# A new order at the beginning of a two-block transformer kernel: mask matmuls ahead, first block by rows, x turned and memory normed behind it

## The chip, the cores and the metric

The kernel runs on one core of one Trainium2 chip. The metric is the device time of one execution in microseconds, the median over runs. Within the core the engines run side by side, each through its own queue in order: TensorE (PE; its weight loads are listed as PEld), VectorE (DVE), ScalarE (ACT), GpSimd (POOL) and SyncE (SP), whose queue here issues the DMAs from memory.

## The reference, cut to what matters

Two transformer blocks over 256 tokens of 1024 features, all in float32. The first block has a mixer of gated branches, a cross attention to a memory of 256 rows, and a mixture of experts; the second block has two more attention layers with rotary positions. The change touches only what stands at the very beginning:

```
h    = rmsnorm(x, norm_mix_g)
proj = h @ w_in                      # a_val, a_gate, u_pool, c_x, c_b, c_c, g
a    = a_val * sigmoid(a_gate)
a    = causal_dwconv(a, conv_a_w) + conv_a_b        # 31 taps
...
k, v = split(rmsnorm(mem, norm_mem_g) @ w_xkv, 2)   # cross attention, needs mem only
x    = x + mixer(h) ; x = x + cross_attention(...) ; x = x + moe(...)
...
cos, sin = rope_tables(positions)    # for the second block
cond     = silu(c)                   # for the second block
```

## The kernel before

Activations are kept with features on the 128 partitions and tokens along the row. Each float32 matmul is done as three matmuls of reduced-precision halves: a weight tile `raw` of 128x1024 comes by DMA, ACT copies it to its high half `whi` (line 99), DVE subtracts to get the low half `wlo` (line 100), and PE multiplies `whi` with the high and the low half of the activation and `wlo` with the high half (lines 141 to 143). A "block" below is one call of `fm_block`: 256 output features from 1024 inputs, 48 matmuls of 128x256, two weight tiles. In the beginning the halves are `hTh`/`hTl` for the normed x and `memTh`/`memTl` for the normed memory.

The order of the program before: x is loaded in two halves of 128 rows and normed (`norm_rows`, line 245 on: squares on ACT into `junk`, the inverse root on ACT and DVE, the scaling on DVE); h is transposed on PE and split into hTh and hTl (lines 554, 555); x itself is transposed as well and copied to `xT` (line 558), which the residual needs much later. Then 72 rows of gains are turned into columns (`gcols`), the memory is loaded, normed and turned by `to_fm` (lines 340 to 344) into memTh and memTl, the positions are loaded and cast (lines 574 to 576), sines and cosines are made, the convolution's 37 rows of constants are turned into `chv`, and four blocks of `w_in` follow. Blocks 1 and 2 give value and gate of the first half (`sg`, line 643, and `apad`, line 644), blocks 3 and 4 those of the second. Each pair starts a convolution `conv` (lines 630, 633), 62 DVE operations on `acv`, that is queued with `later` and stepped by `tick` at each further block. `xkv` then multiplies the normed memory with `w_xkv`.

What sets the order in each engine's queue is a scheduler in the framework: it takes the program in the order written, with the dependencies, priorities by program order and a model of durations, and writes one fixed instruction list for each engine; `behind` adds ordering edges without waits. On the chip nothing is reordered. Weight tiles `raw` and their halves each rotate through 6 buffers (lines 44, 45), the 128x1024 tiles x, h, memx, apad and cpad share four. DMA completions use eight semaphores in turn, so that a DMA is issued only when the eighth before it has landed.

## Time and profile before

| | |
|---|---|
| median of 3 runs | 1216.24 us (1214.25 to 1217.8) |
| profiled execution | 1219.56 us, of which the span is 1217.8 us |
| PE busy | 1175.7 us, 97% of the span |
| DVE busy | 887.5 us, 73% |
| ACT busy | 689.0 us, 57% |
| mean granted TensorE clock | 0.986 |

The profile's times are from the start of the span of one execution, so a row of its timeline can be set against a row of the same execution only. A row of the timeline gives the start, the length, the engine, the line and what is done; "xN" means that N such instructions follow each other and the length is that of all. Durations of neighbours on one engine overlap a little, so the distance of two starts is the better cost of one. In the profile's tables by window, the granted clock is 1.00 at the higher of its two levels (2.4 GHz) and 0.50 at the lower (1.2 GHz).

### The profile page before, as it was taken

How to read it: one execution, taken by the hardware profiler on the slowest of the kernel's cores; microseconds unless marked ns; L12 is line 12 of the kernel's file. 1: busy time of each engine (PE TensorE's matmuls, PEld its weight loads, DVE VectorE, ACT ScalarE, POOL GpSimd, SP SyncE). 2: the span in 40 equal slices, each digit the busy share in tenths (PEclk: the TensorE clock that was granted, in tenths of full speed). 3: DMA queues.
4: the chain of work that ended last, by engine and by line, in shares of the span. 5: the costliest groups of instructions: out<-in, count | busy, mean ns of one | idle time of the engine just before them, and what ended most of it. 6: DMA issues, size and time to landing. Idle time of an engine off the chain costs nothing.

```text
span 1217.8 us, 22374 instructions
## 1 busy us (share of the span) xinstructions
PE 1175.7 (97%) x8690; PEld 1056.2 (87%) x8690; DVE 887.5 (73%) x1649; ACT 689.0 (57%) x1149; POOL 30.7 (3%) x45
## 2 busy tenths in 40 slices
PE   7999999999989999899999999999999989999998
PEld 6989999989868888679667899999977758999998
DVE  7899977666479999697777695578489767654543
ACT  6554357554357777477466475455465555655543
POOL 0000000000000000070000000000010000000000
PEclk8999999999989999999899999999999999999999
DMA  8566565795458999684543597697665346756551
GB/s 253 168 213 190 168 209 167 227 344 184 130 191 286 343 325 359 244 245 161 168 146 122 182 378 240 195 319 268 218 210 182 97 138 208 242 177 196 184 173 36
DMA packets 161310, 258.27 MB, mean 212 GB/s; under 512 B 14255, under 2 KB 106247, under 8 KB 161196
## 3 DMA queue, kind: packets, MB, share of 16 engines
q1 hardware_dynamic: 161196, 256.76, 63.2%
q8 instruction: 70, 1.15, 0.4%
q14 instruction: 44, 0.36, 0.1%
HBM read 255.67 MB, written 1.05 MB: 211 GB/s over the span
## 4 chain that ended last, share of the span: by engine, by line
PE 64%; DVE 4%; DMA 2%; ACT 1%; issue 1%; DVEq 0%; ACTq 0%
PE fm L142 6%; PE fm L143 6%; PE fm L141 6%; PE mo L141 5%; PE mo L142 5%; PE mo L143 5%; PE tm L148 3%; PE tm L150 3%; PE tm L149 3%; PE gu L148 2%; PE gu L149 2%; PE gu L150 2%; PE ada L434 2%; DMA ada<-in_w_ada_dram 2%; PE o L1529 1%; PE py L148 1%
## 5 line engine op out<-in xcount | busy, mean ns | idle before, releaser
L100 DVE TENSOR_TENSOR wlo<-raw,whi 128x1024 fp32r<-128x1024 f32 (+1 forms) x383 | 457.5, 1217 | 167.3 <-ACT whi L99 163.1
L99 ACT ACTIVATE whi<-raw 128x1024 fp32r<-128x1024 f32 (+1 forms) x383 | 392.9, 1049 | 277.4 <-PE fm L142 144.0
L141 PE MATMUL fm<-hTh,whi 128*128 128x256 f32 (+1 forms) x968 | 272.3, 281 | 3.2 <-ACT hTh L217 3.2
L142 PE MATMUL fm<-hTl,whi 128*128 128x256 f32 (+1 forms) x968 | 272.6, 282 | 2.5 <-DVE hTl L555 1.6
L143 PE MATMUL fm<-hTh,wlo 128*128 128x256 f32 (+1 forms) x968 | 271.3, 280 | 0.8 <-DVE wlo L100 0.8
L141 PEld LDWEIGHTS fm<-hTh,whi 128*128 128x128 f32 (+1 forms) x968 | 181.9, 188 | 5.7 <-ACT hTh L217 4.6
L142 PEld LDWEIGHTS fm<-hTl,whi 128*128 128x128 f32 (+1 forms) x968 | 182.2, 188 | 4.6 <-DVE hTl L218 2.5
L143 PEld LDWEIGHTS fm<-hTh,wlo 128*128 128x128 f32 (+1 forms) x968 | 181.9, 188 | 1.1 <-DVE wlo L100 1.0
L142 PE MATMUL mo<-ul,whi 128*128 128x256 f32 x512 | 142.9, 280 | 0.0
L143 PE MATMUL mo<-uh,wlo 128*128 128x256 f32 x512 | 142.8, 280 | 0.0
L141 PE MATMUL mo<-uh,whi 128*128 128x256 f32 x512 | 141.6, 280 | 0.0
L143 PEld LDWEIGHTS mo<-uh,wlo 128*128 128x128 f32 x512 | 96.2, 188 | 0.0
L142 PEld LDWEIGHTS mo<-ul,whi 128*128 128x128 f32 x512 | 96.2, 188 | 0.0
L141 PEld LDWEIGHTS mo<-uh,whi 128*128 128x128 f32 x512 | 95.4, 188 | 0.4 <-issue 0.4
L148 PE MATMUL tm<-whi,hTh 128*128 128x512 f32 x176 | 69.3, 399 | 1.4 <-ACT hsq L907 0.7
L149 PE MATMUL tm<-wlo,hTh 128*128 128x512 f32 x176 | 69.1, 393 | 0.0
L150 PE MATMUL tm<-whi,hTl 128*128 128x512 f32 x176 | 68.0, 392 | 0.3 <-DVE hTl L218 0.3
L141 PE MATMUL fm<-oTh,whi 128*128 128x256 f32 x192 | 54.0, 285 | 2.4 <-ACT oTh L1708 1.4
L142 PE MATMUL fm<-oTl,whi 128*128 128x256 f32 x192 | 54.5, 285 | 0.9 <-DVE oTl L1709 0.8
L143 PE MATMUL fm<-oTh,wlo 128*128 128x256 f32 x192 | 53.1, 279 | 0.0
L633 DVE SCALAR_TENSOR_TENSOR acv<-apad,chv,acv 128x256 f32<-128x256 f32 x120 | 51.5, 478 | 0.0
L148 PE MATMUL gu<-whi,xgh 128*128 128x512 f32 x128 | 50.8, 398 | 0.0
(533 smaller groups left out, 2125.5 us busy)
## 6 DMA issues: line engine op xcount, KB each, us to landing
ada<-in_w_ada_dram SPq DMA_DIRECT2D x96, 512.0 KB, 5.9
raw<-in_w_mlp_in_dram SPq DMA_DIRECT2D x64, 512.0 KB, 6.1
raw<-in_w_mlp_out_dram SPq DMA_DIRECT2D x64, 512.0 KB, 4.3
raw<-in_w_in_dram SPq DMA_DIRECT2D x48, 512.0 KB, 5.1
raw<-in_w_e_down_dram SPq DMA_DIRECT2D x32, 512.0 KB, 4.6
raw<-in_w_e_gate_dram SPq DMA_DIRECT2D x62, 256.0 KB
raw<-in_w_e_up_dram SPq DMA_DIRECT2D x62, 256.0 KB, 4.9
raw<-in_diff_w_in_dram SPq DMA_DIRECT2D x24, 512.0 KB, 3.7
```

The costliest lines, as they stand in the source:

```text
L99: behind("A", SC.activation(hi[:, :n], raw[:, :n], AF.Copy))
L100: last["lo"] = behind("V", V.tensor_tensor(lo[:, :n], raw[:, :n], hi[:, :n].bitcast(F32), op=OP.subtract))
L141: T.matmul(ps, whi[:, c:c + ncol], xh[:, xk, :], start=first, stop=False, **kw)
L142: T.matmul(ps, whi[:, c:c + ncol], xl[:, xk, :], start=False, stop=False, **kw)
L143: return T.matmul(ps, wlo[:, c:c + ncol], xh[:, xk, :], start=False, stop=last, **kw)
L148: T.matmul(ps, xh[:, xk, t0:t0 + P], w[0], start=first, stop=False)
L149: T.matmul(ps, xh[:, xk, t0:t0 + P], w[1], start=False, stop=False)
L150: return T.matmul(ps, xl[:, xk, t0:t0 + P], w[0], start=False, stop=last)
L434: behind("T", T.matmul(ada_part["ps"][32 * j:32 * j + 32, :], w, r[:, S * j:S * j + S], start=start, stop=stop, skip_group_check=True))
L633: V.scalar_tensor_tensor(acv[:, f, :], apad[:, f, j:j + S], chv[:, f, j:j + 1], acv[:, f, :], op0=OP.mult, op1=OP.add)
L1529: T.matmul(o_[64 * hp:64 * hp + 64, :], vTM[:, a, s, gi, :], PT[hp, s, a], start=s == 0 and a == 0, stop=False, skip_group_check=True)
```

## The change

- 32 matmuls of 128x256 of the attention mask `cmask` with the bfloat16 identity, into a bank that nothing reads before it is overwritten, are put on PE ahead of everything else.
- The weight tiles of blocks 1 and 2 are all fetched ahead: one before the constants `col0`, the others right behind. Block 1's second tile is split only after half of hT.
- Block 1 is called with `first=True`: both halves of the output are accumulated row by row of the input (k outside, f inside), so that its first 6 matmuls need only the first row block of hT.
- x is turned into xT no longer ahead of block 1 but in two pieces by `residual`, queued with `later`, behind blocks 2 and 3; its transposes get `behind` edges (`turned` has a new argument `e` for that).
- The DMAs of the memory are written behind the loop over hT, and norm and turn of the memory (`memory`) behind block 1.
- The convolution's constants, `apad`, `conv` and the loop over the four blocks now stand ahead of `bcol`, the positions and sines.

The core of the diff:

```diff
+N_I = 32
...
+            for _ in range(N_I):
+                T.matmul(ada_bank[:, 0, :], identb, cmask, start=True, stop=True)
+            w0 = wmat(win, KD, 0, 256, 0, 1)
             c0_ = cols(16, "col0", vec("norm_mix_g"), vec("c_2"))
-            w0 = wmat(win, KD, 0, 256, 0)
+            w0.fetch(1)
+            w1 = wmat(win, KD, 512, 256, 0, 2)
             for t in range(2):
                 fence["V"] = norm_rows(xr[t], hs[t])
                 fence["A"] = fence["M"]
-            w0.load()
+            w0.load(1)
...
             for c in range(4):
+                if c == 2:
+                    w0.load(1)
                 ps = turned(hs, "hT", c)
...
-            for c in range(4):
-                V.tensor_copy(xT[:, 2 * c:2 * c + 2, :], turned(xr, "fm", c))
-            w1 = wmat(win, KD, 512, 256)
+            for t in range(2):
+                memx[t] = rowt("memx")
+                nc.sync.dma_start(memx[t], A["mem"][0, t * P:(t + 1) * P, :])
...
+            def residual():
+
+                yield
+                for c in range(4):
+                    V.tensor_copy(xT[:, 2 * c:2 * c + 2, :], turned(xr, "fm", c, "T"))
+                    if c % 2:
+                        yield
...
-            for t in range(2):
-                m = rowt("memx")
-                nc.sync.dma_start(m, A["mem"][0, t * P:(t + 1) * P, :])
-                norm_rows(m, m)
-                to_fm(m, aM, t, g_mem)
+            def memory(t):
+                norm_rows(memx[t], memx[t])
+                to_fm(memx[t], aM, t, g_mem)
...
+            for c in range(2):
+                pv = proj(c, None if c else w0, c == 0)
+                if c == 0:
+                    later(residual())
+                    for t in range(2):
+                        memory(t)
+                pg = proj(2 + c, None if c else w1)
+                sg = mx.tile([P, 2, S], F32, tag="sg", name="sg", bufs=4)
+                SC.activation(sg, pg, AF.Sigmoid)
+                V.tensor_tensor(apad[:, 2 * c:2 * c + 2, 30:30 + S], pv, sg, op=OP.mult)
+                later(conv(c))
             bcol = cols(96, "bcol", vec("b_ada_2"))
             pos_i = cp.tile([P, 2], I32, name="pos_i")
```

How the queues look now is shown at three places, before and after the change. First SP, from the first weights to the second set of them. Before, the positions' DMA is issued behind the first four weight tiles:

```order
L93 DMA raw<-in_w_in_dram 128x4x256 x4
L574 DMA pos_i<-in_positions_dram 128x2x1
L603 DMA rows<-in_conv_a_w_dram 31x512
L603 DMA rows<-in_conv_c_w_dram 3x512
L402 DMA rows<-in_norm_mem_g_dram 8x128
```

In the changed kernel the convolution's rows stand there, and the positions come later, behind three more weight tiles and ahead of the memory:

```order
L403 DMA rows<-in_ln_mix_g_dram 16x128
L403 DMA rows<-in_ln_mlp_g_dram 16x128
L593 DMA rows<-in_ln_a_g_dram 1x512
L593 DMA rows<-in_ln_a_b_dram 1x512
L94 DMA raw<-in_w_in_dram 128x4x256 x3
L642 DMA pos_i<-in_positions_dram 128x2x1
L569 DMA memx<-in_mem_dram 128x1024 x2
L861 DMA brt<-in_b_rg_dram 128x4
L94 DMA raw<-in_w_in_dram 128x4x256
L862 DMA brt<-in_b_re_dram 128x16
L94 DMA raw<-in_w_xkv_dram 128x4x256 x3
```

The positions moved from the 9th DMA to the 24th, and the memory from ahead of the second set of weights to behind its first three.

Second, DVE around the cast of the positions (`pos`), which is the instruction that waits for that DMA. Before, it stands behind block 1's two wlo:

```order
L100 TENSOR_TENSOR wlo<-raw,whi 128x1024 x2
L576 CAST pos<-pos_i 128x2
L555 SCALAR_TENSOR_TENSOR hTl<-hT,col_117,hTh 128x256 x3
L580 TENSOR_SCALAR ang<-pos 128x2 x8
L555 SCALAR_TENSOR_TENSOR hTl<-hT,col_117,hTh 128x256 x3
```

In the changed kernel:

```order
L565 SCALAR_TENSOR_TENSOR hTl<-hT,col_153,hTh 128x256
L597 COPY chv<-ax 128x4x37
L644 CAST pos<-pos_i 128x2
L101 TENSOR_TENSOR wlo<-raw,whi 128x1024
L648 TENSOR_SCALAR ang<-pos 128x2 x8
L101 TENSOR_TENSOR wlo<-raw,whi 128x1024 x2
```

The cast went behind the whole of hTl, and the wlo that follows it is now the first of block 2, whose third matmul reads it.

Third, DVE up to the last of the 16 memTl operations. Before, its last 12 rows up to there are:

```order
L100 TENSOR_TENSOR wlo<-raw,whi 128x1024
L630 TENSOR_SCALAR acv<-apad,chv 128x256 x2
L644 TENSOR_TENSOR apad<-fm,sg 128x2x256
L344 SCALAR_TENSOR_TENSOR memTl<-ax,gcols,memTh 128x128
L633 SCALAR_TENSOR_TENSOR acv<-apad,chv,acv 128x256 x2
L630 TENSOR_SCALAR acv<-apad,chv 128x256 x2
L633 SCALAR_TENSOR_TENSOR acv<-apad,chv,acv 128x256
L344 SCALAR_TENSOR_TENSOR memTl<-ax,gcols,memTh 128x128
L633 SCALAR_TENSOR_TENSOR acv<-apad,chv,acv 128x256 x5
L344 SCALAR_TENSOR_TENSOR memTl<-ax,gcols,memTh 128x128
```

In the changed kernel:

```order
L618 TENSOR_SCALAR acv<-apad,chv 128x256 x2
L621 SCALAR_TENSOR_TENSOR acv<-apad,chv,acv 128x256
L701 MEMSET sA 128x4x16
L408 COPY bcol<-ax 128x96
L621 SCALAR_TENSOR_TENSOR acv<-apad,chv,acv 128x256
L345 SCALAR_TENSOR_TENSOR memTl<-ax,gcols,memTh 128x128
L621 SCALAR_TENSOR_TENSOR acv<-apad,chv,acv 128x256 x5
L345 SCALAR_TENSOR_TENSOR memTl<-ax,gcols,memTh 128x128
L621 SCALAR_TENSOR_TENSOR acv<-apad,chv,acv 128x256 x5
L345 SCALAR_TENSOR_TENSOR memTl<-ax,gcols,memTh 128x128
L621 SCALAR_TENSOR_TENSOR acv<-apad,chv,acv 128x256 x5
L345 SCALAR_TENSOR_TENSOR memTl<-ax,gcols,memTh 128x128
```

Of the convolution's operations (acv) 12 stood ahead of the last memTl before, 4 on line 630 and 8 on line 633; now 29 do, 4 and 25. From the wlo that waits for the sine's neighbours on ACT to that last memTl, DVE's list in the changed kernel has 4 wlo, 2 copies to xT, 2 apad, 16 memTl, 29 acv and five small operations.

On ACT the loads of function tables are in another order: before, a table is loaded for sin, then for sgc (the sigmoid of c), and sg follows with that table; in the changed kernel tables are loaded four times in the same stretch, for sg, for r (an exponential, of the memory's norm), for sgc and for sin, and a fifth time for the second sg.

## Rows read from the trace of the kernel before

**Rows 1.** The page: the span, and busy time of PE with its share.

```profile
span 1217.8 us, 22374 instructions
...
PE 1175.7 (97%) x8690; PEld 1056.2 (87%) x8690; DVE 887.5 (73%) x1649; ACT 689.0 (57%) x1149; POOL 30.7 (3%) x45
```

**Rows 2.** Windows: length, PE, PEld, DVE, ACT, POOL busy (count), PE clock, DMA.

```profile
40.00:60.00 20.00, 20.00 (x170) 19.83 (x169) 17.89 (x42) 9.41 (x17) 0.00 (x0) 1.00 0.39 129
...
240.00:260.00 20.00, 20.00 (x180) 18.39 (x182) 9.59 (x14) 7.56 (x11) 0.00 (x0) 1.00 0.95 330
260.00:280.00 20.00, 18.55 (x165) 16.54 (x158) 16.90 (x24) 15.06 (x26) 0.00 (x0) 1.00 1.01 355
```

**Rows 3.** Windows by stage of the beginning.

```profile
12.70:17.20 4.50, 2.14 (x9) 1.67 (x9) 4.50 (x18) 1.92 (x5) 0.00 (x0) 0.57 0.23 65
17.20:20.20 3.00, 3.00 (x16) 3.00 (x16) 2.66 (x18) 2.00 (x4) 0.00 (x0) 0.51 0.85 257
...
31.60:34.41 2.81, 0.16 (x3) 0.04 (x1) 0.87 (x5) 2.78 (x7) 0.00 (x0) 0.89 1.09 348
34.41:37.20 2.79, 2.79 (x13) 2.79 (x14) 2.79 (x5) 2.10 (x5) 0.00 (x0) 0.50 0.62 200
...
47.30:55.00 7.70, 7.70 (x65) 7.70 (x66) 7.61 (x21) 2.10 (x5) 0.00 (x0) 1.00 0.45 145
```

**Rows 4.** Timeline of SP: start, time to issue, DMA.

```profile
4.62 2.29 SPq L574 DMA_DIRECT2D pos_i<-in_positions_dram  x1
...
14.51 0.32 SPq L402 DMA_DIRECT2D rows<-in_ln_mlp_g_dram  x1
...
16.83 2.54 SPq L93 DMA_DIRECT2D raw<-in_w_in_dram  x4
19.42 3.13 SPq L839 DMA_DIRECT2D brt<-in_b_rg_dram  x1
```

**Rows 5.** A wait of SP's queue, 0 to 60 us: total, times, longest.

```profile
SPq L402 <- DMA rows<-in_conv_a_w_dram: 1.2, 1, 1.2
```

**Rows 6.** DMAs issued in 0 to 40 us: count, size, time to landing.

```profile
x<-in_x_dram SPq DMA_DIRECT2D x2, 512.0 KB, 3.5
...
pos_i<-in_positions_dram SPq DMA_DIRECT2D x1, 1.0 KB, 8.2
```

**Rows 7.** Timeline of ACT: start, length, instruction, idle before.

```profile
23.74 1.06 ACT L99 ACTIVATE whi<-raw 128x1024 fp32r<-128x1024 f32 x1 [0.54 <-DMA raw<-in_w_in_dram]
25.25 1.06 ACT L99 ACTIVATE whi<-raw 128x1024 fp32r<-128x1024 f32 x1 [0.44 <-DMA raw<-in_w_in_dram]
...
30.04 0.33 ACT L255 ACTIVATE r<-rv 128x1 f32<-128x1 f32 x2
30.39 1.28 ACT L597 ACT_TABLE_LOAD   x1
31.68 0.21 ACT L597 ACTIVATE sin<-ang 128x16 f32<-128x16 f32 x1
```

**Rows 8.** Timeline of DVE, the same columns.

```profile
14.10 0.17 DVE L576 CAST pos<-pos_i 128x2 f32<-128x2 int32 x1
...
35.41 2.35 DVE L100 TENSOR_TENSOR wlo<-raw,whi 128x1024 fp32r<-128x1024 f32 x2
37.68 0.69 DVE L644 TENSOR_TENSOR apad<-fm,sg 128x512 f32<-128x512 f32 x1
...
38.61 1.59 DVE L344 SCALAR_TENSOR_TENSOR memTl<-ax,gcols,memTh 128x128 fp32r<-128x128 f32 x6
...
51.39 0.73 DVE L630 TENSOR_SCALAR acv<-apad,chv 128x256 f32<-128x256 f32 x2
...
52.69 2.06 DVE L633 SCALAR_TENSOR_TENSOR acv<-apad,chv,acv 128x256 f32<-128x256 f32 x5
54.67 0.34 DVE L344 SCALAR_TENSOR_TENSOR memTl<-ax,gcols,memTh 128x128 fp32r<-128x128 f32 x1
```

**Rows 9.** Timeline of PE: first matmul of xkv, and the first that reads memTl's last row.

```profile
47.34 0.28 PE L141 MATMUL fm<-memTh,whi 128*128 128x256 f32 x1
...
55.25 0.28 PE L142 MATMUL fm<-memTl,whi 128*128 128x256 f32 x1
```

## What the change was predicted to do, before it ran

> **What bounds the kernel now.** I read the page first: PE is busy for 1175.7 of 1217.8 us [rows 1], so the time is PE's work plus the places where PE stands. Then the windows of 20 us: from 40 to 260 us PE shows 20.00 of 20.00 in each of the eleven (the first and the last stand in [rows 2]). So a delay or a gain made in the beginning arrives undiminished at 260 us; in the next window 1.45 us are idle, at a DMA share of 1.01, and over the whole span 42.1 (the difference of the two numbers of the page), the beginning's own with them. The change is worth what it does to the moment at which PE enters its long unbroken stretch.
>
> That moment was read from windows cut by stage. Before, the beginning has three weak places [rows 3]: block 1 starts while hT is still being made (2.14 of 4.50 us busy, granted clock 0.57, then 3.00 us at 0.51); PE stands 2.65 us for the memory's norm; and the 13 instructions behind that run at 0.50. From 47.30 to 55.00 PE is full, and DVE too (7.61 of 7.70). This last row decides: xkv starts at 47.34, the last memTl is computed from 54.67 to 55.01, and the matmul that reads it starts at 55.25 with no idle time before it [rows 8, 9]. DVE delivered it just in time. So I ask when the last memTl comes in the changed kernel, whatever PE gains ahead of it.
>
> **The mask matmuls and block 1 by rows.** The trace has no such matmul of bfloat16. From below they cost nothing (PE waits for x then anyway); from above, 32 matmuls at the distance that fp32r matmuls of this size have at the lower clock: 16 instructions in 3.00 us [rows 3], 0.19 each, 6.0 us. I take 6: from about 2 to 8 us. They may raise the clock by then, but h is ready only after them, so the clock may fall again. x's transposes and copies leave the stretch before block 1, its tiles are split earlier and it needs only one row block of hT to begin: I put its start 1.5 us earlier, at about 11.2, and its end between 20 (all at the higher clock and paced by hTl) and 22, against 23.8 before. Either value is without effect if the next step is right.
>
> **The positions.** DVE's list has the cast of the positions ahead of block 2's first wlo. Before, the cast took 0.17 us and found its data landed [rows 8]; the DMA had been issued at 4.62 and taken 8.2 us, so it landed at 12.8: 1 KB took as long as the four weight tiles queued ahead of it [rows 4, 6]. Now it is the 24th DMA. SP's chain: ln_mlp was issued at 14.51, one of two rows behind a wait for the 31 rows of the convolution [rows 4, 5]; these still land behind the first four tiles, so about 14.2 remains. Four rows of 0.3 to 0.4 us follow, then three weight tiles (4 took 2.54 us [rows 4], 0.5 to 0.6 each): 15.7 to 17.3. The positions' own issue takes 2.29 us: until 19.6. Three tiles of 512 KB are ahead of them, the first landing some 3 us behind its issue (x: 3.5 for two [rows 6]) and the others 1.5 us apart (ACT takes them up at 23.74 and 25.25, both times from a wait for the DMA [rows 7]): 18.8, 20.3, 21.8. The positions land at about 21.9; bounds 19.9 (at once when issued) and 24 (if 256 small pieces take as long again as the issue). The cast and the wlo behind it (2.35 for two [rows 8], so 1.2) end at 23.3. Block 2 was ready to start at 20 to 22 and does its third matmul at 23.3. With 46 matmuls at 0.118 us (65 in 7.70 [rows 3]) block 2 ends at 28.7; 30.8 if the clock is low for a while.
>
> **The sigmoid and the tables.** The first sg stands on ACT behind the whi of a tile of block 3, whose DMA can be issued only when the wlo above has released a buffer, and behind `brt`, 3.13 us of issue [rows 4]: memory's two DMAs until 20.4, `brt` until 23.5, a tile, and then this one at 24.4. It lands at about 28: 21.8 plus four transfers of 1.5 (two of memory, a tile and its own). With whi 1.06, two small operations, 0.6, and a table load of 1.28 [rows 7], sg starts at G = 31.0 to 31.3; bounds 29 and 33. I take 31.3. Behind it on ACT: sg 0.6 (taken a little below apad's 0.69, which has the same size [rows 8]), whi 1.05, load 1.28, r 0.33, load and sgc 1.5, load and sin 1.5, and the first of two whi 1.0. The wlo that DVE does next waits for that whi: G + 7.2 = 38.5. Until then DVE has only the memory's norm left to do, and PE block 3 and the transposes.
>
> Three loads are new in the program. In the trace a load costs its own 1.28 us: r ends at 30.37, the load starts at 30.39, and sin starts at 31.68 [rows 7]. The Trainium skill ("ScalarE: Activation LUTs", section "What ACT_TABLE_LOAD costs") gives 1283 ns for the load and 1380 ns of drain with it, 2.66 us for each switch. By that the four loads up to this point would cost 5.5 us more and the sum would be 1228.5; this trace shows the load's part to within 0.01 us and no drain around it.
>
> **DVE up to the last memTl.** From 38.5 on nothing on DVE's list should wait: what it reads from PE and ACT comes earlier. The work, by distances in [rows 8]: 4 wlo at 1.14 to 1.17, 4.6; two xT copies and two apad at 0.62 (the next row of DVE behind apad), 2.5; 16 memTl at 0.265 (six in 1.59), 4.2; 4 acv of line 630, 0.73 for two less the overlap, 1.3; 25 acv at 0.40 (five in 2.06), 10.0; five small operations, 0.5. Sum 23.1: the last memTl ends at 61.6 instead of 55.01. That is 6.6 us later. The 17 more acv operations that stand ahead of it explain 17 x 0.40 = 6.8 of that by themselves.
>
> PE meanwhile: block 3 from 31.9, the memory's transposes at 38.4, block 4 from 40.3 (its first bank is free when xT is copied) to 46, xkv from there, with the 65 matmuls that don't need the last row until 53.7. So PE enters xkv 1.3 us earlier than before, with 0.85 us of small transposes still to do inside it, and then waits some 7 us in a few pieces, since each of the last three memTl stands behind five acv. Behind the waits nothing gives it back: the acv done early are DVE work saved later, but PE isn't short of DVE there [rows 2]. **Sum:** 6.6 plus 0.2 for the same pick-up as before is +6.8 us. On the profiled execution's 1219.56 that is 1226.4; on the median, 1216.24, which I predict against, **1223.0**. Bounds: G at 29 gives +4.5; G at 33 gives +8.5, and if the clock is at its lower level behind PE's waits, as it was for 2.79 us behind the stall before [rows 3], 1.4 us for each of two such places come on top: +11.3, 1227.5.
>
> **Rivals.**
> 1. *Faster, about 1208.* The three weak places vanish: 25 instructions at 0.118 instead of 7.5 us, less what hTl's pace keeps, 4.1; the stall of 2.8; 1.3 from transposes at full clock [rows 3]. That is 8.2 us. It needs the last memTl at 47, or at 51.6 for a gain of 0.3%; by DVE's 30.3 us from G, that is G at or below 21.3. For it: PE's weak places are real and the program addresses each. Against it: raw tiles that land at 1.5 us each and the positions behind them put G eight us later.
> 2. *No change, about 1216.* Landings are earlier than I think and the small DVE operations cheaper, so that the last memTl comes at about 55 (G at 24.7), or PE's later waits take up the shift. Against it: the bound of 29 for G, and only 1.45 us idle in the first window that has any [rows 2].
> 3. *Slower still, about 1228 to 1232*: the positions land at 24 or later and a low clock follows each wait, or each table load holds ACT for longer than its own 1.28 us, say as long again: four of them are 5.1 us, 1228.1. [Rows 7] speak against the second. The page of the Trainium skill named above says about that much.
> 4. *The mask matmuls don't do what they are for*: done at 8 us, the clock is back at the lower level when block 1 starts. That costs 2 to 3 us in block 1 and nothing in the sum, as PE waits for DVE until 23.3 in any case.
>
> **How the numbers follow.** My forecast (with 4 in it) 0.66, rival 1 0.12, rival 2 0.16, rival 3 0.06. A measurement of this kernel can tell 0.3%, 3.65 us, from no change. The forecast's own range, 1220.7 to 1227.5, lies above 1219.9, with 0.02 of its chance left below that; so slower has 0.64 + 0.06 = 0.70, the same 0.16 + 0.02 = 0.18, and faster 0.12. The range leaves out rival 1's deeper gains and most of rival 3: 1212.5 to 1228.5.
>
> **What would show it.** In the profile after: a wait of DVE for the positions' DMA ahead of a wlo near 22 us, and PE waiting for that wlo at block 2's third matmul; table loads four times between about 29 and 37; PE idle inside xkv, released by memTl, three times or more, 6 to 8 us in all, and the last memTl at about 61.5. If the cast doesn't wait, or G lies before 27, the chain is wrong at its start; if the last memTl comes at 55 or earlier, it is wrong in DVE's sum. A PE that is full in xkv would refute it.

## The result, and the profile after

The changed kernel takes 1227.21 us (median of 6 runs, 1225.59 to 1229.88); the kernel before 1215.53 (6 runs, 1211.51 to 1220.67). The two medians lie 11.7 us apart. The ratio that the text goes by is not their quotient (1.0096) but 1.0077, with a 95% interval of 1.0056 to 1.0097: slower by about 9.4 us. The profiled executions differ by 8.07 (1227.63 against 1219.56). The forecast was 1223.0 with a range of 1212.5 to 1228.5, and slower at 0.70.

The page of the kernel after; to be set against [rows 1]. The span grew by 8.1 us and PE's busy time by 3.9, but the masks' 5.1 us are in the busy time, in a stretch in which PE waited for x for about half of the time before. Without them PE is busy for 1.2 us less than before, so the loss is PE standing and not PE working for longer:

```profile
span 1225.9 us, 22435 instructions
...
PE 1179.6 (96%) x8722; PEld 1058.0 (86%) x8722; DVE 887.7 (72%) x1649; ACT 693.1 (57%) x1152; POOL 30.7 (3%) x45
```

Windows of the kernel after, with the columns of [rows 2]. The window 40 to 60, which was full, now has 3.51 us idle, and the next one 1.81. The idle time at 260 to 280 is 1.45 us as before: nothing is given back there.

```profile
40.00:60.00 20.00, 16.49 (x131) 15.32 (x130) 19.66 (x51) 10.97 (x24) 0.00 (x0) 1.00 0.38 125
60.00:80.00 20.00, 18.19 (x147) 17.70 (x147) 20.00 (x42) 9.82 (x13) 0.00 (x0) 1.00 0.34 104
...
260.00:280.00 20.00, 18.55 (x174) 15.15 (x174) 12.03 (x23) 11.51 (x23) 0.00 (x0) 1.00 0.96 334
```

What matters is when xkv is through. The next row is the list of one tile's instructions (memTh) on PE: one of xkv's three matmuls in each step, with the shortest, median and longest duration in ns, then the start of the first and of the last. First the kernel before:

```profile
L141 PE MATMUL fm<-memTh,whi x64: 280/283/283, 47.3 to 70.0; 128*128 128x256 f32 x64
```

Then the kernel after:

```profile
L142 PE MATMUL fm<-memTh,whi x64: 278/283/387, 49.2 to 79.1; 128*128 128x256 f32 x64
```

So xkv starts 1.9 us later and lasts 29.9 us instead of 22.7; its last step comes 9.1 us later. Of the longer 7.2 us, 5.0 are PE's waits for sg and memTl. The rest is in part the four transposes of memx put in between (0.60 us) and the slower first matmul behind each wait; I didn't break it down further. PE's timeline of the kernel after shows the masks, block 2's third matmul and two of xkv's waits (start, length, instruction, idle time before it and what ended it):

```profile
2.13 5.12 PE L537 MATMUL ada<-cmask,identb 128*128 128x256 bf16 x32 [2.13 <-DVE identb L386]
...
26.17 0.58 PE L144 MATMUL fm<-hTh,wlo 128*128 128x256 f32 x1 [5.39 <-DVE wlo L101]
...
52.60 0.39 PE L142 MATMUL fm<-memTh,whi 128*128 128x256 f32 x1 [1.40 <-ACT sg L635]
...
64.24 0.39 PE L143 MATMUL fm<-memTl,whi 128*128 128x256 f32 x1 [0.91 <-DVE memTl L345]
```

The list of waits, 0 to 70 us, gives the sums (total, times, longest):

```profile
DVE pos L644 <- DMA pos_i<-in_positions_dram: 6.1, 1, 6.1
...
PE fm L143 <- DVE memTl L345: 3.6, 5, 0.9
```

DVE's timeline of the kernel after, which answers to [rows 8]: the cast that waits for the positions, the wlo behind it, the memory's scaling, the wlo from which the sum ran, and the last convolution ahead of the last memTl.

```profile
24.81 0.17 DVE L644 CAST pos<-pos_i 128x2 f32<-128x2 int32 x1 [6.09 <-DMA pos_i<-in_positions_dram]
24.89 1.23 DVE L101 TENSOR_TENSOR wlo<-raw,whi 128x1024 fp32r<-128x1024 f32 x1
...
39.07 0.17 DVE L671 TENSOR_TENSOR cond<-col,sgc 128x8 f32<-128x8 f32 x1 [1.26 <-ACT sgc L670]
...
39.46 1.67 DVE L260 TENSOR_SCALAR memx<-memx,r 128x512 f32<-128x512 f32 x4
...
41.55 1.23 DVE L101 TENSOR_TENSOR wlo<-raw,whi 128x1024 fp32r<-128x1024 f32 x1 [0.34 <-ACT whi L100]
...
61.85 2.07 DVE L621 SCALAR_TENSOR_TENSOR acv<-apad,chv,acv 128x256 f32<-128x256 f32 x5
63.83 0.36 DVE L345 SCALAR_TENSOR_TENSOR memTl<-ax,gcols,memTh 128x128 fp32r<-128x128 f32 x1
```

ACT's row for the third of the three tiles that are fetched ahead of the positions, then its row for the whi ahead of sg, then ACT between sg and the whi for which that wlo waits: the four loads and what they stand ahead of.

```profile
24.14 1.06 ACT L100 ACTIVATE whi<-raw 128x1024 fp32r<-128x1024 f32 x1 [2.49 <-DMA raw<-in_w_in_dram]
...
31.62 1.06 ACT L100 ACTIVATE whi<-raw 128x1024 fp32r<-128x1024 f32 x1 [1.63 <-PE fm L143]
...
33.07 1.28 ACT L635 ACT_TABLE_LOAD   x1
34.37 0.60 ACT L635 ACTIVATE sg<-fm 128x512 f32<-128x512 f32 x1
...
35.93 1.28 ACT L256 ACT_TABLE_LOAD   x1
37.22 0.29 ACT L256 ACTIVATE r<-rv 128x1 f32<-128x1 f32 x2
37.54 1.28 ACT L670 ACT_TABLE_LOAD   x1
38.83 0.21 ACT L670 ACTIVATE sgc<-col 128x8 f32<-128x8 f32 x1
39.06 1.28 ACT L665 ACT_TABLE_LOAD   x1
40.35 0.22 ACT L665 ACTIVATE sin<-ang 128x16 f32<-128x16 f32 x1
```

SP's queue up to the positions (start, time to issue; to be set against [rows 4]), and then windows: the transfers between 11 and 17 us, and the two stretches at the lower clock, block 1's beginning and block 2 behind the wait.

```profile
10.28 0.27 SPq L403 DMA_DIRECT2D rows<-in_norm_f_g_dram  x1
11.75 0.27 SPq L403 DMA_DIRECT2D rows<-in_pool_scale_dram  x1
14.00 0.32 SPq L403 DMA_DIRECT2D rows<-in_ln_mix_g_dram  x1
...
15.44 1.49 SPq L94 DMA_DIRECT2D raw<-in_w_in_dram  x3
16.97 0.52 SPq L642 DMA_DIRECT2D pos_i<-in_positions_dram  x1
17.58 0.94 SPq L569 DMA_DIRECT2D memx<-in_mem_dram  x2
```

```profile
11.00:17.00 6.00, 5.75 (x33) 5.41 (x34) 4.52 (x11) 4.60 (x10) 0.00 (x0) 0.72 0.11 32
...
12.00:15.00 3.00, 2.87 (x14) 2.80 (x14) 2.65 (x6) 2.65 (x6) 0.00 (x0) 0.50 0.05 17
...
26.00:29.00 3.00, 2.83 (x13) 2.83 (x14) 3.00 (x13) 2.72 (x9) 0.00 (x0) 0.50 0.83 256
```

The last number of a window's row is GB/s: for six microseconds, in block 1, hardly anything was transferred (32). SP's rows show why: each small row is issued when the eighth DMA before it has landed. For the rows at 10.28 and 11.75 that is a weight tile, one every 1.5 us; for the row at 14.00 it is the convolution's 31 rows. All tiles issued so far had landed near 11, and the next one was issued at 15.44. The kernel before has this hole too, with 79 GB/s from 11 to 17 us.

### The profile page after: what moved, and what is told of

The parts are those of the page before. It is cut to its first block, busy times and chain, and to the rows that moved or that the text cites. A ratio compares the mean times of both kernels' runs of the same rounds, so it can differ in the third digit from the quotient of the medians.

```text
span 1225.9 us, 22435 instructions
## 1 busy us (share of the span) xinstructions
PE 1179.6 (96%) x8722; PEld 1058.0 (86%) x8722; DVE 887.7 (72%) x1649; ACT 693.1 (57%) x1152; POOL 30.7 (3%) x45
## 4 chain that ended last, share of the span: by engine, by line
PE 61%; DVE 5%; issue 2%; DMA 2%; ACT 2%; SPq 0%; DVEq 0%; ACTq 0%
PE fm L143 6%; PE fm L144 6%; PE fm L142 6%; PE mo L142 5%; PE mo L143 5%; PE mo L144 5%; PE tm L149 3%; PE tm L151 3%; PE tm L150 3%; PE gu L149 2%; PE gu L150 2%; PE gu L151 2%; PE ada L435 1%; DMA ada<-in_w_ada_dram 1%; DVE wlo L101 1%
```

## The experiments

Every kernel of the experiments ran beside the kernel before on the same chip. "xkv" is the start of the first and of the last of its 64 steps in the profile, as in the two rows above; it comes from a single profiled execution of each kernel. Such times differ by about 1 us between kernels whose lists are the same up to there: sg starts at 34.37 in the changed kernel and at 33.20 in conv_behind.

| run | xkv, us | last memTl starts | ratio to before, 95% interval |
|---|---|---|---|
| before | 47.3 to 70.0 | 54.67 | 1 |
| after | 49.2 to 79.1 | 63.83 | 1.0077 (1.0056 to 1.0097) |
| no_mask | 48.8 to 78.5 | 63.28 | 1.0086 (1.0059 to 1.0113) |
| pos_early | 48.7 to 78.7 | 62.80 | 1.009 (1.0062 to 1.0118) |
| mem_tables | 48.4 to 76.9 | 61.60 | 1.0062 (1.0043 to 1.008) |
| mem_late | 47.6 to 76.6 | 59.90 | 1.0054 (1.0033 to 1.0074) |
| conv_behind | 48.0 to 71.3 | 54.52 | 1.0041 (1.0022 to 1.006) |
| pos_conv | 50.1 to 73.3 | 56.34 | 1.0035 (1.0019 to 1.0052) |
| full | 48.0 to 71.2 | 53.54 | 1.0014 (1.0 to 1.0028) |
| full2 | 45.8 to 69.1 | 52.05 | 0.9997 (0.9982 to 1.0012) |
| full4 | 40.3 to 63.5 | 46.25 | 0.995 (0.993 to 0.9969) |
| full4_nomask | 41.7 to 64.9 | 47.63 | 0.9972 (0.9958 to 0.9986) |
| before_mask | 45.1 to 67.8 | 52.39 | 0.9995 (0.9978 to 1.0012) |
| before_small | 43.7 to 68.6 | 53.32 | 1.0007 (0.9995 to 1.0019) |

Divided by 1216, the shift of xkv's last step gives the ratio to within 0.2 points in 12 of the 13 rows (after: 9.1 us, 0.75%; mem_late: 6.6, 0.54%; full4: -6.5, -0.53%). Only conv_behind stands 0.3 points above it. In conv_behind and before_small the shift lies outside the ratio's interval. An early start of xkv counts for nothing by itself: before_small starts it 3.6 us earlier and takes 1.0007.

Four of the rows form a square. Putting the convolution behind memTl takes 0.36 points off the changed kernel (after to conv_behind) and 0.40 off mem_late (mem_late to full). The edits of mem_late, which put the memory ahead, take 0.23 off the changed kernel (after to mem_late) and 0.27 off conv_behind (conv_behind to full). Both together take 0.63 of the 0.77 points, about the sum of the two. The smaller steps by themselves are no wider than the intervals.

**1. The positions' DMA early (pos_early).** Only the place of that one DMA changes: from behind the second set of tiles to right behind the first four.

```diff
             w1 = wmat(win, KD, 512, 256, 0, 2)
+            pos_i = cp.tile([P, 2], I32, name="pos_i")
+            ...
+                nc.sync.dma_start(pos_i, ...)
...
             bcol = cols(96, "bcol", vec("b_ada_2"))
-            pos_i = cp.tile([P, 2], I32, name="pos_i")
-            ...
-                nc.sync.dma_start(pos_i, ...)
```

> The changed kernel with one edit: the DMA of the positions is issued right behind the first four weight tiles, as before the change. Theory A (a chain: the positions' landing holds DVE at the cast, so block 2, the first sigmoid and DVE's run to the last memTl all come later; then 29 convolution operations stand ahead of the last memTl): the cast no longer waits (6.1 us in the changed kernel), block 2 starts at about 20.8 without the 5.4 us of waiting, the first sigmoid starts near 30 instead of 34.4, the last memTl ends near 60 instead of 64.2, and the time is 3 to 4.5 us below the changed kernel's, about 1223. Rival B (the convolution ahead of memTl is all that counts, the cast's wait is hidden by DMA landings further on): the last memTl stays at 63 to 64 and the time within 1 us of the changed kernel's, 1226 to 1228. Rival C (the clock: block 2 and the waits inside xkv at a lower clock): time as in A only if the granted clock of 26 to 29 us, 0.50 in the changed kernel, is 1.00.

The cast ran at 12.95 us, PE's wait of 5.4 us at block 2 was gone, and sg started at 31.94 instead of 34.37. The time didn't get better: 1.009, as rival B said, though not for its reason. DVE's timeline and PE's waits in this run show what came next:

```profile
38.27 0.17 DVE L671 TENSOR_TENSOR cond<-col,sgc 128x8 f32<-128x8 f32 x1 [2.88 <-ACT sgc L670]
...
62.80 0.35 DVE L345 SCALAR_TENSOR_TENSOR memTl<-ax,gcols,memTh 128x128 fp32r<-128x128 f32 x1
```

```profile
PE ax L341 <- DVE memx L260: 3.9, 1, 3.9
```

The memory is scaled behind a wait for sgc, which stands on ACT behind sg and three more loads, and PE stands 3.9 us for it. Most of the time won at one gate was lost at the next. The wait that the forecast began with is real, and taking it away alone was worth nothing.

**2. The convolution behind memTl (conv_behind).** Ordering edges alone: each half's first acv comes behind the last memTl, with the positions as late as in the changed kernel.

```diff
-                V.scalar_tensor_tensor(lo[:, k, ts], ...
+                fence["C"] = V.scalar_tensor_tensor(lo[:, k, ts], ...
...
-                            V.tensor_scalar(acv[:, f, :], ...
+                            behind("C", V.tensor_scalar(acv[:, f, :], ...
```

> The changed kernel with one edit: the first operation of each half of the convolution gets an ordering edge behind the last memTl, so that DVE's list has all 29 of them behind it. Theory A: up to the first sigmoid nothing changes (it starts near 34.4), then the last memTl ends 7 to 9 us earlier, near 56, xkv runs from about 50 without its five waits for memTl (3.6 us) and the pieces behind; the shift against the kernel before shrinks from 8 to about 3 us, less what comes back as waits for wlo between 60 and 160 us, where DVE now has 17 to 29 operations (7 to 11 us) more to do: 1218 to 1222. Rival B: all of the loss is the convolution, 1215 to 1217. Rival D (DVE is the bound up to 160 us anyway, so that what is put off there comes back in full): 1225 to 1228, with PE idle for wlo between 60 and 160 us.

The last memTl came 9.3 us earlier than in the changed kernel, and xkv's last step 7.8 earlier, with no wait for memTl in it. About 1.2 us of both were there already at sg, where the two lists are still the same. The edit also moves all 29 acv, not only the 17 that the change had put ahead. The time fell by about half of the loss: 1.0041, against 1.0077. Some of the rest was given back where the convolution's result is needed; a wait appears there that the changed kernel doesn't have. The window and the list of waits (200 to 260 us) of this run:

```profile
200.00:220.00 20.00, 18.51 (x158) 18.30 (x158) 17.48 (x22) 14.91 (x19) 0.00 (x0) 1.00 0.65 200
```

```profile
PE fm L142 <- ACT aLh L218: 1.5, 1, 1.5
```

With xkv's last step 1.3 us behind that of the kernel before, that makes 1.3 + 1.5 = 2.8 us, 0.23%, in this profile; the measured 0.41% has an interval from 0.22 to 0.60.

**3. Both (pos_conv).** The two edits above together.

```diff
             w1 = wmat(win, KD, 512, 256, 0, 2)
+            pos_i = cp.tile([P, 2], I32, name="pos_i")
...
+                            behind("C", V.tensor_scalar(acv[:, f, :], ...
```

> Both edits in the changed kernel: the positions' DMA early, and the convolution behind the last memTl. Theory A: the two add up; the first sigmoid near 30, xkv from about 46 without waits, and so 1 to 2 us ahead of the kernel before: 1213 to 1216. Rival D (put-off convolution work comes back as waits for wlo): 1219 to 1223. Rival E (what block 1 and 2 gain ahead is never worth anything): same as the kernel before within 1 us.

Measured 1.0035, no better than conv_behind alone. PE stood 3.2 us for a copy to xT and 3.9 us for memx. So the expected gain was missed: with both of my causes gone, the memory's norm was a gate as in 1.

**4. Without the masks (no_mask).**

```diff
-N_I = 32
+N_I = 0
```

> The changed kernel with the 32 mask matmuls left out (their results are never read). The scheduler's lists differ from the changed kernel's in one more thing: DVE's cast of the positions stands behind four wlo instead of ahead of them. Theory A: the mask matmuls are worth nothing at the end, since block 2 waits for DVE in any case; without them block 1 is slower (granted clock 0.50 for longer, end at 22 to 23 instead of 20.8), but block 2 no longer waits for the positions, and the time falls by 1 to 4 us against the changed kernel's: 1223 to 1226. Rival F (the mask matmuls bring the part of the start that is gained, and the cast costs little): 1228 to 1231.

Measured 1.0086, the same as after within the intervals; the 1 to 4 us that I expected to gain didn't come. In DVE's list of this kernel the cast stands behind four wlo, so block 2 isn't the same; the last memTl at 63.28 shows that neither matters to the end.

**5. Two table loads fewer (mem_tables).** sg is ordered behind the memory's r.

```diff
-                SC.activation(sg, pg, AF.Sigmoid)
+                behind("M", SC.activation(sg, pg, AF.Sigmoid))
```

> The changed kernel with one edit: the sigmoid sg gets an ordering edge behind r (the exponential of the memory's norm), so that ACT loads no table between them: two loads between 30 and 41 us instead of four. After the first four runs I hold that the gate behind the positions' wait is the memory's norm on ACT (its r stands behind sg and two table loads, memx is scaled only at 39.5). Theory G (that gate): memx is scaled 1.3 to 2.6 us earlier, the last memTl ends at 62 instead of 64.2, the time is 1.5 to 2.5 us below the changed kernel's: ratio to the kernel before 1.005 to 1.007. Rival B (only DVE's convolution ahead of memTl counts): ratio unchanged, 1.0075.

The last memTl came 2.2 us earlier (61.60) and xkv's last step too; 1.0062. The memory was scaled 1.2 us earlier (38.27 against 39.46). The tables explain no more than that, and the two ratios' intervals overlap.

**6. The memory's norm ahead of everything (mem_late).** The memory's DMAs go ahead of the second set of tiles, sg behind the memory's r, and the cast behind the last memTl.

```diff
-            last["w"] = nc.sync.dma_start(view(raw), src)
+            last["w"] = behind("X", nc.sync.dma_start(view(raw), src))
...
-                nc.sync.dma_start(memx[t], ...
+                fence["X"] = nc.sync.dma_start(memx[t], ...
...
+                behind("M", SC.activation(sg, pg, AF.Sigmoid))
...
-            V.tensor_copy(pos, pos_i)
+            behind("C", V.tensor_copy(pos, pos_i))
```

> The changed kernel with the memory ahead (its DMAs are issued ahead of the second set of weight tiles, sg behind r) and the cast of the positions behind the last memTl; the convolution stays mixed into memTl. Theory G: both gates ahead of DVE's run are gone, memx is scaled near 28, PE has no wait of more than 3 us before xkv, the last memTl ends near 57; still some waits for memTl inside xkv. Ratio 1.000 to 1.004. Rival B: last memTl near 63, ratio 1.007. Rival H (the weight tiles, which now land 3 us later behind memory, are the gate): block 3 starts no earlier than 33 and the ratio is 1.005 or more.

Measured 1.0054, outside the 1.000 to 1.004 of theory G and near rival H. The memory is ready early, but 1 MB goes ahead of the tiles. PE now stands 5.1 us for sg (start 31.55), which is on ACT behind the whi of tiles that land late, and block 3 starts at 32.18.

**7. With the convolution behind (full).** The edits of 6 and 2.

```diff
+            last["w"] = behind("X", nc.sync.dma_start(view(raw), src))
...
+                behind("M", SC.activation(sg, pg, AF.Sigmoid))
...
+                            behind("C", V.tensor_scalar(acv[:, f, :], ...
```

> As mem_late, with the convolution behind the last memTl too: none of the three waits is left. Theory G with A: xkv starts near 42 and runs without a wait, 5 us ahead of the kernel before; DVE has 12 operations of the convolution (4.8 us) more to do behind that point than the kernel before, and gives back 0 to 4 us in waits for wlo. Ratio 0.996 to 1.000, 1211 to 1216 against 1216. Rival D (put-off convolution comes back in full): ratio 1.002 to 1.004, with PE waiting for wlo between 60 and 200 us.

Measured 1.0014: this order gives back most of the loss and gains nothing; xkv started at 48.0, not near 42. PE's wait for sg was 4.9 us, and the five microseconds from 31 on ran at the lower clock. The windows of this run point to a cause 15 us earlier, which 9 and 10 test: 32 and 20 GB/s between 11 and 19 us, with room for the missing tiles.

```profile
11.00:14.00 3.00, 2.46 (x16) 1.94 (x17) 2.11 (x6) 2.85 (x7) 0.00 (x0) 1.00 0.10 32
14.00:19.00 5.00, 4.39 (x37) 4.04 (x37) 3.76 (x9) 3.13 (x6) 0.00 (x0) 1.00 0.27 20
31.00:36.00 5.00, 4.22 (x19) 4.22 (x20) 5.00 (x9) 2.62 (x4) 0.00 (x0) 0.50 1.09 348
```

**8. The masks in the kernel before (before_mask).**

```diff
+N_I = 32
...
+            for _ in range(N_I):
+                T.matmul(ada_bank[:, 0, :], identb, cmask, start=True, stop=True)
```

> The kernel before with one part of the change: the 32 mask matmuls ahead of everything. Theory (mask matmuls end near 8 us and the clock falls again while hT is made): x's transposes go 1 to 2 us later, block 1 still runs partly at the lower clock; the memory's norm sets when block 3 goes on, so nothing is gained at the end: ratio 0.999 to 1.002. Rival: block 1 at the higher clock ends 2 to 3 us earlier and xkv starts as much earlier: ratio 0.997 to 0.998.

Measured 0.9995: no change to be told. Block 1 still waits 1.8 us for hTl. In the profile xkv ends 2.2 us earlier, which is 0.18%; the interval has room for that.

**9. Block 3's tiles ahead too (full2).** full, with two more tiles fetched at the start.

```diff
+            w2 = wmat(win, KD, 256, 256, 0, 2)
...
-                pv = proj(c, None if c else w0, c == 0)
+                pv = proj(c, w2 if c else w0, c == 0)
```

> full with one more edit: block 3's two weight tiles are fetched right behind block 2's, ahead of the small rows. In full PE stands 4.9 us ahead of block 3 for a sigmoid that stands behind a weight tile on ACT, while the DMA engines move 1 to 54 GB/s from 11 to 19 us (350 before and behind): SP's queue is held by the small rows, each waiting for the eighth DMA before it. Theory I (that hole in the DMA stream is what keeps the beginning from being shorter, in all versions): two tiles (3 us) fill part of the hole, block 3 starts near 28 instead of 31.8, xkv 3 to 4 us earlier than the 47.6 of full: ratio 0.996 to 0.999. Rival J (DVE is the bound once the waits are gone): xkv starts earlier, but PE waits for memTl or wlo up to 200 us instead: ratio 1.000 to 1.002.

Measured 0.9997, short of the 0.996 to 0.999 of theory I. The wait for sg is gone, but the hole in the transfers only moved: 331 GB/s from 11 to 14 us, then 32 from 14 to 21. PE now stands for the small rows themselves and for xT (list of waits, 8 to 66 us):

```profile
PE fm L142 <- DVE xT L576: 2.5, 1, 2.5
PE ax L406 <- DMA rows<-in_ln_a_b_dram: 2.1, 1, 2.1
```

**10. The small rows on GpSimd's queue (full4).** full2, with the 12 row DMAs of `gcols` and of the convolution issued on GpSimd's queue instead of SP's. Same data, same transfers.

```diff
-    def cols(n, name, *parts):
+    def cols(n, name, *parts, q=nc.sync):
...
-            nc.sync.dma_start(rows[r0:r0 + ap.shape[0], :], ap)
+            q.dma_start(rows[r0:r0 + ap.shape[0], :], ap)
...
+                      q=nc.gpsimd)
...
-                nc.sync.dma_start(rows[r0:r0 + n, :], A[nm][0])
+                nc.gpsimd.dma_start(rows[r0:r0 + n, :], A[nm][0])
...
-                nc.sync.dma_start(rows[r0:r0 + 1, :], A[nm])
+                nc.gpsimd.dma_start(rows[r0:r0 + 1, :], A[nm])
```

> full2 with the convolution's and the gains' rows (12 small DMAs) issued by GpSimd's queue instead of SP's, so that SP is not held by them. Theory I: the DMA engines are busy from 11 to 19 us, memory lands 2 to 4 us earlier, PE has less than 2 us of waits between block 1 and xkv, xkv starts near 41: ratio 0.993 to 0.997. Rival J: 0.999 to 1.002. Rival K (GpSimd's issuing delays the identity that PE's transposes need, or its rows come late): PE waits at the start for the identity or in block 1 for rows, ratio as full2 or more.

Measured 0.995 (0.993 to 0.9969), 1213.29 us against 1218.76: it beats both kernels. In this run's windows the hole is gone, the memory's DMAs are issued at 14.30 instead of 19.19, and the clock is at its higher level all through block 1. The identity did come later, as rival K feared: the masks start at 3.38 instead of 2.13, at no cost that shows. GpSimd's timeline shows what a row costs to issue there.

```profile
11.00:14.00 3.00, 2.17 (x14) 1.66 (x15) 2.39 (x7) 2.56 (x6) 0.00 (x0) 1.00 1.11 344
14.00:21.00 7.00, 7.00 (x62) 6.83 (x61) 5.65 (x10) 5.65 (x9) 0.00 (x0) 1.00 0.99 323
```

```profile
7.77 0.50 POOL L403 DMA_DIRECT2D rows<-in_norm_x_g_dram  x1
```

```profile
L142 PE MATMUL fm<-memTh,whi x64: 280/283/286, 40.3 to 63.5; 128*128 128x256 f32 x64
```

From 8 to 66 us PE's longest wait is 0.5 us. Full2 against full4 is the cleanest comparison of the set: one edit to queues, 5.6 us at xkv, 0.47 points.

**11. The same edit in the kernel before (before_small).**

```diff
+            q.dma_start(rows[r0:r0 + ap.shape[0], :], ap)
...
+                      q=nc.gpsimd)
...
+                nc.gpsimd.dma_start(rows[r0:r0 + n, :], A[nm][0])
...
+                nc.gpsimd.dma_start(rows[r0:r0 + 1, :], A[nm])
```

> The kernel before, with its 12 small row transfers (norm columns and convolution rows) issued on GpSimd's queue and nothing else changed: no masks, the old order of block 1, memory and x. Theory I (the hole in the transfers at 12 to 17 us, in which SyncE's queue is held by small rows, is what the beginning pays for): tiles and memory land some 3 us earlier, the hole is filled to above 150 GB/s, the first xkv stands near 42 to 44 us, and the ratio is 0.996 to 0.999. Rival: the kernel before is held in its first 50 us by VectorE's own work, so what lands earlier only waits: ratio 0.999 to 1.001, xkv unmoved.

The rival was right about the time, 1.0007, and the theory about the path: the hole was filled (344 GB/s from 11 to 17 us, against 79), the stall ahead of memx was gone, and xkv started 3.6 us earlier. But the last memTl, which now stands behind 15 acv on DVE, came only 1.35 us earlier, and xkv waited 0.9 us for it. DVE's row and the row of xkv in this run:

```profile
53.32 0.35 DVE L344 SCALAR_TENSOR_TENSOR memTl<-ax,gcols,memTh 128x128 fp32r<-128x128 f32 x1
```

```profile
L141 PE MATMUL fm<-memTh,whi x64: 278/283/384, 43.7 to 68.6; 128*128 128x256 f32 x64
```

**12. full4 without the masks (full4_nomask).**

```diff
-N_I = 32
+N_I = 0
```

> The best order so far (row block by row block, memory normed ahead of sg, convolution behind memory's turns, block 3's tiles ahead, small rows on GpSimd's queue) with the 32 masks taken out. Theory: once the gates behind block 1 are gone, block 1's speed counts; without masks it runs longer at 1.2 GHz and what stands behind it comes 1 to 2 us later, 0.996 of the kernel before instead of 0.995. Rival: the masks change nothing, since the rows and the tiles set the time of block 1: ratio within 0.001 of 0.995.

Measured 0.9972 (0.9958 to 0.9986). In the profiles xkv comes 1.4 us later than with the masks. The two profiles part ahead of xkv at block 1 and the transposes before it: in block 1 neighbouring matmuls stand 0.21 us apart without masks until 16.3 us, and 0.12 apart with them. PE's timeline without masks:

```profile
13.12 0.41 PE L144 MATMUL fm<-hTh,wlo 128*128 128x256 f32 x1
13.33 0.41 PE L142 MATMUL fm<-hTh,whi 128*128 128x256 f32 x1
```

And with them:

```profile
12.71 0.28 PE L144 MATMUL fm<-hTh,wlo 128*128 128x256 f32 x1
12.82 0.28 PE L142 MATMUL fm<-hTh,whi 128*128 128x256 f32 x1
```

Here the masks do raise the clock in time. The two ratios differ by 0.22 points, but they were taken on different chips and their intervals overlap by 0.11, so the size of the gain isn't settled.

## Why the prediction was right, point by point

**What decides.** "The change is worth what it does to the moment at which PE enters its long unbroken stretch": read as the end of xkv, this held in 11 of the 13 runs, where the ratio's interval holds the shift; before_small shows that an earlier start of xkv isn't enough. In the changed kernel the last memTl decided, as the prediction said. With the convolution behind it PE no longer waits for memTl, and what decides is when xkv can start.

**The mask matmuls and block 1.** "The trace has no such matmul of bfloat16" was a misreading: the kernel before has the same matmul of `cmask` and the identity on line 1481, 32 times (from the list of PE's groups by line):

```profile
L1481 PE MATMUL s<-cmask,identb 128*128 128x256 bf16 x32 | 8.7, 282 | 0.0
```

Where two of them follow each other, they stand 0.12 us apart at a granted clock of 1.00; 32 at that distance are 3.8 us. The forecast took the distance at the lower clock and put them at 6.0 us, from about 2 to 8; measured 5.12, from 2.13 to 7.25. Block 1 began at 11.7 (forecast 11.2) and ended inside the forecast's 20 to 22. Rival 4 came true in this profile: by 12 us the clock was back at its lower level for three microseconds. It doesn't belong to the order. In the eight other profiles of the changed order with masks, from pos_early to full4, the clock reads 1.00 from 12 to 15 us, with neighbours 0.12 us apart. For the changed kernel's time the masks made no difference that can be told, as no_mask shows.

**The positions.** This is where the sizes were off. The landing was put at 21.9, with 24 as the upper bound; the cast started at 24.81. One guess was wrong in the good direction: the issue took 0.52 us and not the 2.29 of [rows 4], so that DMA was out at 17.5 and not at 19.6. The other was wrong by more: I counted the three tiles ahead of the positions at 1.5 us each. ACT took up the first two at 19.11 and 20.60, but it waited for the third until 24.14, and not until 21.8; the positions landed right behind it, as assumed. From 16 to 22 us the transfers ran at 268 GB/s. That is 1.6 MB, as much as the three tiles hold, and the third was still not there, so some of it was probably the memory's 1 MB, queued behind them. No run tests this. The positions took 7.8 us from their issue, close to the 8.2 of [rows 6]. The bound from that row (17.0 + 8.2 = 25.2) would have been the better value to take.

**Block 2 and G.** PE's third matmul waited 5.39 us, as the mechanism said, until 26.17 instead of 23.3. Then it ran at the lower clock for about 3 us, which was the 30.8 that I had named and not taken. Together these put block 2's end near 33.1 and sg at G = 34.37 instead of 31.3, past the upper bound of 33. The tile that I thought would hold sg wasn't late: that whi, at 31.62, waited for PE to free its buffer and not for a DMA.

**From G on** the terms held. The wlo that starts the sum came at 41.55, which is G + 7.18 (forecast 7.2). From there to the end of the last memTl at 64.19 DVE needed 22.6 us (forecast 23.1). The four loads cost 1.28 us each with the next operation 0.01 to 0.02 us behind. The Trainium skill ("ScalarE: Activation LUTs", section "What ACT_TABLE_LOAD costs") adds a drain of 1380 ns to each switch. The trace after doesn't show it either.

**The sum.** The last memTl ended 9.2 us later than before, not 6.6; the profiled execution was 8.1 longer. The forecast of +6.8 lies at the lower end of what was measured (0.56 to 0.97%, 6.8 to 11.8 us). The missing part is G's 3.1 us less 0.5 from DVE's sum; 1.1 us came back later, at a place that I didn't find. The median, 1227.21, lies at the top of the forecast's own range (1227.5). One sign was missed in size: PE's waits for memTl in xkv were 3.6 us in five pieces, not 6 to 8, because xkv started at 49.2 and not at 46.

**The causes, weighed by the runs.** "The 17 more acv operations that stand ahead of it explain 17 x 0.40 = 6.8 of that by themselves" was the strongest sentence: conv_behind changed that order alone, and the last memTl came at 54.52, where the kernel before has it (54.67). In time this was worth 0.36 points, about half of the loss, and by the square above the edits of mem_late take off more than half of the rest. The chain that led there was weaker than I made it. The prediction treats the positions as the cause of a late G; pos_early shows that a second gate, the memory's norm behind sg, its tables and sgc, stood right behind it and would have given nearly the same time. So the direction was earned, but the size came near in part by luck: the sum runs through a wait whose removal changed nothing. And one thing that bears on both wasn't in the prediction at all. The change needs more tiles earlier, and for six microseconds hardly anything is transferred. The kernel before has the hole too, so it can't explain the loss by itself; that the loss has its root there is argued and not shown. [Rows 5] showed 1.2 us of SP's wait for the small rows; I read it as a date in the chain of SP, and not as six microseconds of lost transfers. The change's ideas are all in full4, at 0.995; what failed was its order of the memory's norm and the convolution, and the queue that it left as it was.

**The rivals.** Rival 1 asked for G at or below 21.3 and 1208 us; G came 13 us later. Its condition rests on DVE's order: in full4 sg starts at 29.05, and the last memTl ends at 46.60, since no acv stands ahead of it. Rival 2 fell with the last memTl at 64.2. Rival 3 came true in part: the positions landed later than 24, and the clock was low for 3 us behind PE's wait at block 2. But it stayed at 1.00 behind the waits in xkv, and the loads came without drain. By the ratio the time is 1225.6 (1216.24 x 1.0077), 2.6 above the forecast and 2.4 below this rival's range; by the median it is nearer to the rival. Its chance of 0.06 looks too small.

Open: whether the masks are worth 0.2%, why conv_behind measured 0.18 points more than its profile accounts for, whether full4's gain needs the memory's place, since the rows were never moved alone in the changed kernel, and whether the rows, issued behind the tiles on SP's own queue, would do as well.

## What to carry to other kernels

When work is moved earlier in a kernel whose engines run fixed lists, look for the instruction that stands behind it on the engine with the least room: here 29 convolution operations on VectorE, waited for only past 200 us when they were put off, stood ahead of the last operation that the next 23 us of TensorE needed. Take away one gate and expect the next; a wait's length in the trace says little about what is won without it (5.4 us here, for nothing). And before reordering the consumers, read GB/s in steps of a microsecond: a hole in the first 20 us, with large loads queued behind small ones, was worth 0.47 points (full2 to full4), while the reordering without it only came back to the kernel before. It was worth nothing where DVE's order still stood in front of it (before_small).

## What the runs showed of the hardware

- 1 KB of positions, 256 values of 4 bytes, landed some 8 us after its issue, behind weight tiles of 512 KB: 8.2 in the kernel before, 7.8 up to the cast in the changed one, 8.1 in pos_early, 7.9 in full4. Its issue took 2.29 us in the kernel before and 0.52 in the changed one.
- Moving 12 row DMAs, of some 110 KB together, to GpSimd's queue raised the transfers from 32 to 323 GB/s between 14 and 21 us (full2 against full4); issuing one costs GpSimd 0.50 us. The Trainium skill ("DMA: Bandwidth & Descriptors", section "Issuing engines are not separate DMA queues") says that all queues share the same 16 engines and interleave whichever engine issued. The rate from 8 to 11 us agrees: 353 GB/s in the kernel before and 356 in full2 with one queue, 357 in before_small and 347 in full4 with two. What the second queue saved was SP's waiting: the memory's DMAs were issued 4.9 us earlier.
- The granted clock's column can read 1.00 where the pace says otherwise: in full4_nomask it is 1.00 from 10 to 16 us, with matmuls of 256 columns 0.21 us apart, as in the changed kernel's stretch at 0.50. In no_mask it is the same at 12 us. There the distance of neighbours tells more.
